# Attention's value products turned round, and the convolution's taps shared out anew, in a two-layer encoder kernel

## The chip, the cores and the metric

The kernel runs on one core of a Trainium2 chip. The metric is the device time of one execution in microseconds; the time before is the median of three runs. Engines go by their profile names: PE is TensorE (PEld its weight loads), DVE VectorE, ACT ScalarE, POOL GpSimd, SP SyncE, which here only issues transfers.

## What is computed

Two layers of a streaming encoder, on 512 tokens of 1024 features in float32. Each layer is a half-step feed-forward block, a mixing block, another half-step feed-forward block and a norm. The change lies in the mixing block:

```
h = rms_norm(x);  p = h @ w_in            # columns split among the two groups
group A: 8 heads of latent attention, q and k 96 wide, v 64 wide, block-causal mask
   probs = softmax(scores);  out = probs @ v
group B: u = a * sigmoid(g)               # 512 channels
   y = causal depthwise convolution of u, 31 taps, + bias
   conv = silu(layer_norm(y))
x = x + concat(attn, conv) @ w_out
```

So an output of the convolution at token t is the sum over s = 0..30 of tap s times u at token t - s, channel by channel.

## The kernel before

Features lie on the 128 partitions and the 512 tokens along the free axis, so x is eight tiles of 128 x 512. Large products are made in three passes over a high and a low part of both operands (`mm3`, L153 to L157). The order on each engine is set by a planner, which lists the instructions by simulated readiness and by their order in the program; `issue_after` adds constraints. Each engine then works through its list strictly in order.

The mixing block is `mix_body` (L617). It goes through these stages, all tiles of the step in one pass:
- The gated input u of the four convolution groups of 128 channels (`conv_in`, `glu`), the latent projections, queries and keys. `SEQ` (L44) gives their order; groups 2 and 3 come last. Weights come by SP's queue into three `raw` buffers, and ACT and DVE (or POOL) cut them into parts (`load_w`, L134).
- Attention (L808 to L908), a software pipeline over eight heads (`ORDER`, L59): `turn` transposes q and k; `scores` makes scores, maxima and exponentials for four blocks of 128 queries; `turn_p` transposes the probabilities, so that keys lie on the partitions; `values` (L861) takes each transposed 128 x 128 block of probabilities as the stationary operand and streams 64 value columns past it, ten products a head. An odd head then scales its pair by the reciprocal sums (L875), and `turn_out` (L879) transposes the pair's result back to features and splits it (L161, L162).
- The convolution (L913 to L933). `CONV = "DAAD"`: groups 0 and 3 lie on DVE, each tap one fused multiply-add in a PSUM tile `cv` (L922), copied back by ACT (L932). In groups 1 and 2 ACT makes the product of each tap (L926) and POOL adds it (L930). Only taps below `PAUSE` of group 1 may be added before the keys are done. These taps are spread by the planner among the attention's instructions.
- The layer norm over the 512 channels (L943 to L967): POOL sums the four groups (L944 to L946), a product with a constant matrix gives the mean of each token (L948), the groups are centred and squared, `token` and `spread` give the reciprocal deviation on all partitions (L198, L217), and the swish and the split give the four convolution operands.
- The output projection (L969 to L980). Its attention half can start without the convolution: `early_groups` (L936) fills PE during the layer norm. `E1 = 0`, `E2 = 2`, `E3 = 3` say how many of the early output columns come before the mean, before the norm's token sums and before the spread; `WOG = 3` is the number of output tiles worked on together. `WOP = 4` output weights are loaded during the attention.

SBUF tiles come from pools with a fixed number of buffers: `ring` (35 tiles of 128 x 512), `tmps` (5), the block's own `m` (12) and `y` (2), and seven PSUM banks beside `cv`.

Of the kernel before, what the change touches and what calls it, by code (L numbers as in the profile page):

```python
# [7 lines left out]
FP = mybir.dt.float32  # L8
# [17 lines left out]
DV = 64  # L26
# [3 lines left out]
CK = 31  # L30
# [29 lines left out]
JOINED = ("b21", "t3", "t4")  # L60

VECS = [("g1", 8), ("gm", 8), ("g2", 8), ("gp", 8), ("gql", 3), ("gkl", 2),
        ("cw", 4 * CK), ("cb", 4), ("lg", 4), ("lb", 4), ("gq", 1), ("gk", 1)]
VOFF = {}
_o = 0
for _n, _w in VECS:
# [1 line left out]
    _o += _w  # L68
VN = _o
CCOS, CSIN, CID = 0, 64, 128  # L70
CN = 256


@with_exitstack
def encoder_kernel(ctx: ExitStack, tc: tile.TileContext, xT, consts, vecs, rgain, wgu1, wd1, wdq1,
                   wcv, wql, wkl, wuq, wkv, wout, wgu2, wd2, wdq2, out):
    nc = tc.nc
# [18 lines left out]

    def bank():
        return psum.tile([P, S], FP, tag="ps", name=nm("ps"))
# [13 lines left out]
    ident = cst[:, CID:CID + P]  # L112
# [17 lines left out]
    def vv(l, name):  # L130
        o, w = VOFF[name]
        return vec[:, l, o:o + w]
# [18 lines left out]
    order = {}  # L151
# [7 lines left out]
    def split(src, made=slot):  # L159
        hi, lo = made(FR), made(FR)  # L160
        order["high"] = A.copy(hi, src).ins  # L161
        order["evicted"] = V.tensor_tensor(lo, src, hi.bitcast(FP), ALU.subtract).ins  # L162
        return hi, lo
# [452 lines left out]

    def mix_body(kpool, l, gx, norm, done):  # L617
        u, order = [], {}

        def kept(dt=FP):  # L620
            return kpool.tile([P, S], dt, tag="m", name=nm("m"), bufs=2 * WIDE)
        ys = [None if kind == "D" else kpool.tile([P, S], FP, tag="y", name=nm("y"), bufs=2) for kind in CONV]

        def glu(pa, pg):
            tg = tmp()
            V.tensor_tensor(tg, pg, R, ALU.mult)
            sg = tmp()
            order["gate"] = A.activation(sg, tg, AF.Sigmoid).ins
            ta = tmp()
            V.tensor_tensor(ta, pa, R, ALU.mult)  # L630
            uc = kept()
            (G if GLUP else V).tensor_tensor(uc, ta, sg, ALU.mult)
# [12 lines left out]
        stq = Stats()  # L645
        cqT, ckT, pq, scqs, vs = [], [], [], [], []
# [214 lines left out]
        def values(h):  # L861

            if h % 2 == 0:
                heads[h]["po"] = bank()
            po = heads[h - h % 2]["po"].rearrange("p (t h d) -> p t h d", t=NT, h=2)
            for t in range(NT):
                for j in range(t + 1):
                    T.matmul(po[:, t, h % 2], heads[h]["pt"][j][:, (t - j) * P:(t - j + 1) * P],  # L868
                             vs[j][:, h * DV:(h + 1) * DV], start=j == 0, stop=j == t)
# [5 lines left out]
            V.tensor_tensor(o.rearrange("p (t h d) -> p t h d", t=NT, h=2), po,  # L875
                            rs[:, :, :, None].to_broadcast([P, NT, 2, DV]), ALU.mult)
            heads[h]["o"] = o

        def turn_out(h):  # L879

            if h % 2 == 0:
                return
            o = heads[h]["o"]
            ps = bank()
            for t in range(NT):
                T.transpose(ps[:, t * P:(t + 1) * P], o[:, t * P:(t + 1) * P], ident)
# [9 lines left out]
        with tc.issue_after(order["turned"]):  # L896
            for t in range(NT):
                ps = up_kv(wv, t)
                v = kept()
                V.tensor_scalar(v, ps, sk[:, t:t + 1], None, ALU.mult)  # L900
                vs.append(v)
        with tc.issue_after(order["gate"]):
            scores(0)
        for step in range(H + 6):
            for stage, lag in STAGES:
                h = step - lag
                if 0 <= h < H and not (stage is turn and h < AHEAD or stage is scores and h == 0):
                    stage(h)  # L908
# [5 lines left out]
        for c in range(4):  # L914
            kind = CONV[c]
            acc = psum.tile([P, S], FP, tag="cv", name=nm("cv"), bufs=1) if kind == "D" else ys[c]
            tap = lambda k: cw[:, c * CK + k:c * CK + k + 1]
            A.activation(acc, u[c], AF.Identity, scale=tap(CK - 1), bias=cb[:, c:c + 1])  # L918
            for k in range(CK - 2, -1, -1):
                s = CK - 1 - k  # L920
                if kind == "D":
                    V.scalar_tensor_tensor(acc[:, s:], u[c][:, :S - s], tap(k), acc[:, s:], ALU.mult, ALU.add)  # L922
                    continue
                pr = kpool.tile([P, S], FP, tag="pr", name=nm("pr"), bufs=3)
                if kind == "A":
                    A.activation(pr[:, s:], u[c][:, :S - s], AF.Copy, scale=tap(k))  # L926
                else:
                    G.tensor_scalar(pr[:, s:], u[c][:, :S - s], tap(k), None, ALU.mult)
                with tc.issue_after(order["keys"]) if s >= PAUSE or c > 1 else nullcontext():
                    order["conv"] = G.tensor_tensor(acc[:, s:], acc[:, s:], pr[:, s:], ALU.add).ins  # L930
            if kind == "D":
                A.copy(u[c], acc)  # L932
                ys[c] = u[c]  # L933
        early = []

        def early_groups(ms):  # L936
# [9 lines left out]
        (G if YP else V).tensor_tensor(ysum, ysum, ys[3], ALU.add)  # L946
        pm = bank()
        T.matmul(pm, onesm, ysum, start=True, stop=True)  # L948
        if PRELOAD:
# [6 lines left out]
        r = st.token(CW)  # L956
        early_groups(range(E2, E3))
        pr = spread(r)
        early_groups(range(E3, WOG))
        lg, lb = vv(l, "lg"), vv(l, "lb")  # L960
        cv = []
        for c in range(4):
            z = tmp()
            V.tensor_tensor(z, ys[c], pr, ALU.mult)
            s = tmp()
# [275 lines left out]
```

## Time and profile before

| | |
|---|---|
| median of three runs | 1798.41 us (1798.37 to 1800.6) |
| profiled execution | 1798.87 us |
| its span on the core | 1797.1 us |
| granted TensorE clock | 1.0 |
| first mixing block, attention to convolution operands | about 450 to 521.5 us from the span's start |
| second mixing block, the same | about 1340 to 1411.5 us |

The profiled execution is one run with the hardware profiler on. A group row reads: line, engine, operation, output<-inputs, shape and count, then the busy time in us, the mean duration of one in ns, and the engine's idle time in us just before these instructions with what ended it. For PE the shape begins with rows*columns of the weight tile. Durations on PE run from entering the array to leaving it, so they overlap. A row of the chain in order of time reads: start, length, engine, tile and line, count.

### The profile page before, as it was taken

How to read it: one execution, taken by the hardware profiler on the slowest of the kernel's cores; microseconds unless marked ns; L12 is line 12 of the kernel's file. 1: busy time of each engine (PE TensorE's matmuls, PEld its weight loads, DVE VectorE, ACT ScalarE, POOL GpSimd, SP SyncE). 2: the span in 40 equal slices, each digit the busy share in tenths (PEclk: the TensorE clock that was granted, in tenths of full speed). 3: DMA queues.
4: the chain of work that ended last, by engine and by line, in shares of the span. 5: the costliest groups of instructions: out<-in, count | busy, mean ns of one | idle time of the engine just before them, and what ended most of it. 6: DMA issues, size and time to landing. Idle time of an engine off the chain costs nothing.

```text
span 1797.1 us, 29235 instructions
## 1 busy us (share of the span) xinstructions
PE 1781.8 (99%) x11334; PEld 1602.4 (89%) x11334; DVE 1494.5 (83%) x2299; ACT 1107.5 (62%) x1721; POOL 421.5 (23%) x343
## 2 busy tenths in 40 slices
PE   9999999999999999999999999999999999999998
PEld 7899999888788899999888999998978788999997
DVE  7898988589956989898779989876998668989883
ACT  5575756457953575756645757554779435756564
POOL 1000000258943000000310000002689410000002
PEclk9999999999999999999999999999999999999999
DMA  5657575325103466665426575743250125575742
GB/s 168 171 131 182 135 177 123 109 88 134 33 22 102 123 164 161 155 160 132 123 65 170 122 194 122 193 112 111 81 147 7 46 82 160 140 183 134 182 117 74
DMA packets 70413, 226.16 MB, mean 126 GB/s; under 512 B 7937, under 2 KB 8321, under 8 KB 70273
## 3 DMA queue, kind: packets, MB, share of 16 engines
q1 hardware_dynamic: 54000, 169.74, 30.3%
q0 software_dynamic: 16128, 54.53, 18.0%
q8 instruction: 89, 1.46, 0.3%
q14 instruction: 52, 0.42, 0.1%
q10 hardware_dynamic: 144, 0.00, 0.0%
HBM read 222.15 MB, written 2.10 MB: 125 GB/s over the span
## 4 chain that ended last, share of the span: by engine, by line
PE 91%; ACT 3%; DVE 2%; POOL 2%; issue 1%; DMA 0%; SPq 0%; ACTq 0%; POOLq 0%; DVEq 0%
PE ps L154 24%; PE ps L156 23%; PE ps L155 23%; PE ps L373 11%; PE ps L374 6%; PE ps L868 1%; PE ps L834 1%; POOL y L930 1%; ACT pr L926 1%; ACT r L840 1%; PE ps L855 1%; PE ps L198 0%; POOL sck L173 0%; PE ps L217 0%; DVE wl L246 0%
## 5 line engine op out<-in xcount | busy, mean ns | idle before, releaser
L155 PE MATMUL ps<-r,wh 128*128 128x256 f32 (+1 forms) x2540 | 806.8, 318 | 0.0
L154 PE MATMUL ps<-r,wh 128*128 128x256 f32 (+1 forms) x2540 | 803.6, 320 | 2.2 <-ACT wh L138 0.7
L156 PE MATMUL ps<-r,wl 128*128 128x256 f32 (+1 forms) x2348 | 749.2, 321 | 0.0
L154 PEld LDWEIGHTS ps<-r,wh 128*128 128x128 f32 x2540 | 480.5, 189 | 47.0 <-ACT wh L138 3.6
L155 PEld LDWEIGHTS ps<-r,wh 128*128 128x128 f32 x2540 | 481.6, 190 | 35.8 <-DVE r L162 1.5
L156 PEld LDWEIGHTS ps<-r,wl 128*128 128x128 f32 x2348 | 445.1, 190 | 33.5 <-DVE wl L144 0.4
L373 PE MATMUL ps<-xj,wh 128*128 128x512 f32 x864 | 303.9, 392 | 0.0
L138 ACT CAST wh<-raw 128x1024 fp32r<-128x1024 f32 (+3 forms) x148 | 131.9, 899 | 208.1 <-PE ps L155 125.8
L390 POOL DMA_DIRECT2D ls<-in_wgu x72 | 62.7, 871 | 734.7 <-ACT ls L389 595.3
L244 ACT CAST wh<-fr 128x1024 fp32r<-128x1024 f32 (+1 forms) x160 | 157.6, 985 | 104.4 <-DVE fr L410 53.2
L144 DVE TENSOR_TENSOR wl<-raw,wh 128x1024 fp32r<-128x1024 f32 (+3 forms) x132 | 145.3, 1108 | 91.3 <-ACT wh L138 90.9
L246 DVE TENSOR_TENSOR wl<-fr,wh 128x1024 fp32r<-128x1024 f32 (+1 forms) x160 | 182.3, 1139 | 20.3 <-ACT wh L244 20.3
L373 PEld LDWEIGHTS ps<-xj,wh 128*128 128x128 f32 x864 | 161.4, 188 | 30.1
L930 POOL TENSOR_TENSOR y<-y,pr 128x511 f32<-128x511 f32 (+14 forms) x120 | 158.6, 1322 | 54.5 <-ACT pr L926 47.1
L374 PE MATMUL ps<-xj,ls 128*128 128x256 f32 x576 | 161.3, 280 | 0.0
L244 ACT CAST wh<-raw 128x1024 fp32r<-128x1024 f32 (+1 forms) x100 | 98.2, 982 | 45.1 <-PE ps L155 24.2
L246 DVE TENSOR_TENSOR wl<-raw,wh 128x1024 fp32r<-128x1024 f32 (+1 forms) x100 | 113.5, 1135 | 14.2 <-ACT wh L244 13.7
L191 POOL TENSOR_TENSOR r<-r,t 128x512 f32<-128x512 f32 x45 | 75.0, 1676 | 175.6 <-ACT t L187 174.8
L374 PEld LDWEIGHTS ps<-xj,ls 128*128 128x128 f32 x576 | 108.3, 188 | 0.0
L389 ACT ACTIVATE ls<-fr 128x1024 fp32r<-128x1024 f32 (+1 forms) x56 | 56.1, 1002 | 74.5 <-PE ps L374 42.8
L926 ACT ACTIVATE pr<-m,vec 128x511 f32<-128x511 f32 (+14 forms) x120 | 85.7, 736 | 13.2 <-POOL y L930 13.2
L922 DVE SCALAR_TENSOR_TENSOR cv<-m,vec,cv 128x511 f32<-128x511 f32 (+14 forms) x120 | 87.8, 732 | 3.6 <-ACT cv L918 2.2
(241 smaller groups left out, 2944.9 us busy)
## 6 DMA issues: line engine op xcount, KB each, us to landing
fr<-in_wgu SPq DMA_DIRECT2D x112, 512.0 KB, 4.2
ls<-in_wgu POOLq DMA_DIRECT2D x72, 512.0 KB, 6.2
raw<-in_wgu SPq DMA_DIRECT2D x62, 512.0 KB, 4.5
fr<-in_wdq SPq DMA_DIRECT2D x48, 384.0 KB, 4.6
ls<-in_wdq POOLq DMA_DIRECT2D x32, 384.0 KB, 4.8
raw<-in_wd SPq DMA_DIRECT2D x32, 384.0 KB, 3.2
raw<-in_wd SPq DMA_DIRECT2D x32, 256.0 KB, 2.8
raw<-in_wcv SPq DMA_DIRECT2D x16, 512.0 KB, 3.6
```

Of the source, the lines that this page charges most:

```text
L138: order["cast"] = A.copy(hi[:, :w], raw[:, :w]).ins
L144: (G if kind in POOLW.split() else V).tensor_tensor(lo[:, :w], raw[:, :w], hi[:, :w].bitcast(FP), ALU.subtract)
L154: T.matmul(o, lh, rh, start=first, stop=False, skip_group_check=free)
L155: T.matmul(o, lh, rl, start=False, stop=False, skip_group_check=free)
L156: order["mm"] = T.matmul(o, ll, rh, start=False, stop=last, skip_group_check=free).ins
L244: A.copy(hi[:, :w], src[:, :w])
L246: order["lo"] = V.tensor_tensor(lo[:, :w], src[:, :w], hi[:, :w].bitcast(FP), ALU.subtract).ins
L373: T.matmul(o, w[0][:, c], both, start=start and k == 0, stop=False, skip_group_check=True)
L374: last = T.matmul(o[:, 0:HS], w[1][:, c], both[:, 0:HS], start=False, stop=k == 3, skip_group_check=True).ins
L922: V.scalar_tensor_tensor(acc[:, s:], u[c][:, :S - s], tap(k), acc[:, s:], ALU.mult, ALU.add)
L926: A.activation(pr[:, s:], u[c][:, :S - s], AF.Copy, scale=tap(k))
L930: order["conv"] = G.tensor_tensor(acc[:, s:], acc[:, s:], pr[:, s:], ALU.add).ins
```

## The change

- **Values.** `values` now handles a pair of heads at its odd head. The value tile of a head (64 columns) is the stationary operand and the transposed probabilities stream past it: 4 products a head of 512, 384, 256 and 128 columns. The two heads write partitions 0 to 63 and 64 to 127 of one bank, in alternation. The result has features on the partitions at once, so the four transposes in `turn_out` go. The reciprocal sums are needed along the free axis then: 8 products of a broadcast column with the identity spread them, ACT copies them to SBUF, and DVE multiplies.
- **Taps.** `TAPS = (0, 31, 31, 9)` gives for each group the number of taps that are not on DVE. Group 0 is on DVE as before, group 1 on ACT and POOL. Of group 2 (`PC`) the first 16 taps (`PT`) go to PE and 15 stay on ACT and POOL. Of group 3 the first 9 taps go to ACT and POOL and 22 stay on DVE in `cv`, begun by an ACT copy and added to the group by DVE at the end.
- **Taps on PE.** For 32 channels at a time, four copies of u shifted by 0 to 3 tokens are brought by 4 transfers on SP's queue into one 128-row tile (16 transfers a layer). `diag` holds the taps as 32-column diagonal blocks, made by POOL. `conv_pe` makes 16 products of 500 to 512 columns, in four 32-row parts of one bank, in alternation, and ACT adds the bias. It stands ahead of pipeline step 3 (`PSTEP`).
- **Smaller edits.** The last add of the layer norm's sum goes from POOL to DVE. `E1` is 1 and `WOG` 4: one early column before the mean, two before the token sums, three before the spread and a fourth after it, and the output tiles go four and four. Pool `m` has 11 buffers, `y` 3; three of the four pairs' results take ring tiles, before it was two.

```diff
-CONV = "DAAD"
+TAPS = (0, 31, 31, 9)
+Q = 32
+PT = 16
+PC = 2
+PSTEP = 3
...
-E1 = 0
-YP = 1
+E1 = 1
 E2 = 2
 E3 = 3
-WOG = 3
+WOG = 4
...
+        diag = kpool.tile([P, PT, Q], FP, tag="m", name=nm("m"), bufs=11)
+        G.tensor_tensor(diag, cst[:, None, CI32:CI32 + Q].to_broadcast([P, PT, Q]),
+                        vv(l, "cp")[:, :, None].to_broadcast([P, PT, Q]), ALU.mult)
+        shifted = []
...
             glu(*pp)
+            if c != PC:
+                return
+            for i in range(4):
+                v = slot()
+                V.memset(v[:, 0:4], 0.0)
+                for r in range(4):
+                    nc.sync.dma_start(out=v[r * Q:(r + 1) * Q, r:], in_=u[c][i * Q:(i + 1) * Q, 0:S - r])
+                shifted.append(v)
+
+        def conv_pe():
+
+            ps = bank()
+            for a in range(PT // 4):
+                for i in range(4):
+                    T.matmul(ps[i * Q:(i + 1) * Q, 4 * a:], diag[:, 4 * a + i], shifted[i][:, 0:S - 4 * a],
+                             start=a == 0, stop=a == PT // 4 - 1)
+            A.activation(ys[PC], ps, AF.Identity, bias=vv(l, "cb")[:, PC:PC + 1])
...
             if h % 2 == 0:
-                heads[h]["po"] = bank()
-            po = heads[h - h % 2]["po"].rearrange("p (t h d) -> p t h d", t=NT, h=2)
-            for t in range(NT):
-                for j in range(t + 1):
-                    T.matmul(po[:, t, h % 2], heads[h]["pt"][j][:, (t - j) * P:(t - j + 1) * P],
-                             vs[j][:, h * DV:(h + 1) * DV], start=j == 0, stop=j == t)
-            if h % 2 == 0:
                 return
             rs = small.tile([P, NT, 2], FP, tag="rs", name=nm("rs"))
             V.reciprocal(rs, heads[h - 1]["sums"])
+            pr = bank()
+            for t in range(NT):
+                for i in range(2):
+                    T.matmul(pr[i * DV:(i + 1) * DV, t * P:(t + 1) * P], rs[:, t, i:i + 1].to_broadcast([P, DV]),
+                             ident, start=True, stop=True)
+            r = tmp()
+            A.copy(r, pr)
+            po = bank()
+            for j in range(NT):
+                for i in range(2):
+                    T.matmul(po[i * DV:(i + 1) * DV, j * P:], vs[j][:, (h - 1 + i) * DV:(h + i) * DV],
+                             heads[h - 1 + i]["pt"][j], start=j == 0, stop=j == NT - 1)
             o = tmp()
-            V.tensor_tensor(o.rearrange("p (t h d) -> p t h d", t=NT, h=2), po,
-                            rs[:, :, :, None].to_broadcast([P, NT, 2, DV]), ALU.mult)
+            V.tensor_tensor(o, po, r, ALU.mult)
...
-            ps = bank()
-            for t in range(NT):
-                T.transpose(ps[:, t * P:(t + 1) * P], o[:, t * P:(t + 1) * P], ident)
-            at.append(split(ps, kept if len(at) < 2 else slot))
+            at.append(split(heads[h]["o"], kept if len(at) < 1 else slot))
...
+            if step == PSTEP:
+                conv_pe()
...
+            acc = psum.tile([P, S], FP, tag="cv", name=nm("cv"), bufs=1) if n < CK else None
+            if n and c != PC:
+                A.activation(ys[c], u[c], AF.Identity, scale=tap(CK - 1), bias=cb[:, c:c + 1])
+            for s in range(n, CK):
+                k = CK - 1 - s
+                if s == 0:
+                    A.activation(acc, u[c], AF.Identity, scale=tap(k), bias=cb[:, c:c + 1])
+                elif s == n:
+                    A.activation(acc[:, s:], u[c][:, :S - s], AF.Copy, scale=tap(k))
+                else:
                     V.scalar_tensor_tensor(acc[:, s:], u[c][:, :S - s], tap(k), acc[:, s:], ALU.mult, ALU.add)
+            for s in range(PT if c == PC else 1, n):
...
+                A.activation(pr[:, s:], u[c][:, :S - s], AF.Copy, scale=tap(k))
                 with tc.issue_after(order["keys"]) if s >= PAUSE or c > 1 else nullcontext():
-                    order["conv"] = G.tensor_tensor(acc[:, s:], acc[:, s:], pr[:, s:], ALU.add).ins
-            if kind == "D":
+                    order["conv"] = G.tensor_tensor(ys[c][:, s:], ys[c][:, s:], pr[:, s:], ALU.add).ins
+            if not n:
                 A.copy(u[c], acc)
                 ys[c] = u[c]
+            elif n < CK:
+                V.tensor_tensor(ys[c][:, n:], ys[c][:, n:], acc[:, n:], ALU.add)
...
-        (G if YP else V).tensor_tensor(ysum, ysum, ys[3], ALU.add)
+        V.tensor_tensor(ysum, ysum, ys[3], ALU.add)
```

More of the change, by code (lines that the diff above doesn't have):

```diff
@@ L70 @@
 CCOS, CSIN, CID = 0, 64, 128
-CN = 256
+CI32 = 256
+CN = 288
 @with_exitstack
@@ L618, in mix_body @@
         u, order = [], {}
+        diag = kpool.tile([P, PT, Q], FP, tag="m", name=nm("m"), bufs=11)
+        G.tensor_tensor(diag, cst[:, None, CI32:CI32 + Q].to_broadcast([P, PT, Q]),
+                        vv(l, "cp")[:, :, None].to_broadcast([P, PT, Q]), ALU.mult)
+        shifted = []
         def kept(dt=FP):
-            return kpool.tile([P, S], dt, tag="m", name=nm("m"), bufs=2 * WIDE)
-        ys = [None if kind == "D" else kpool.tile([P, S], FP, tag="y", name=nm("y"), bufs=2) for kind in CONV]
+            return kpool.tile([P, S], dt, tag="m", name=nm("m"), bufs=11)
+        ys = [kpool.tile([P, S], FP, tag="y", name=nm("y"), bufs=3) if n else None for n in TAPS]
         def glu(pa, pg):
@@ L913, in mix_body @@
         cw, cb = vv(l, "cw"), vv(l, "cb")
[L914 to L916 removed]
+        for c, n in enumerate(TAPS):
             tap = lambda k: cw[:, c * CK + k:c * CK + k + 1]
[L918 to L921 removed]
+            acc = psum.tile([P, S], FP, tag="cv", name=nm("cv"), bufs=1) if n < CK else None
[8 more added lines that the diff above has]
+                else:
                     V.scalar_tensor_tensor(acc[:, s:], u[c][:, :S - s], tap(k), acc[:, s:], ALU.mult, ALU.add)
[L923 removed]
+            for s in range(PT if c == PC else 1, n):
+                k = CK - 1 - s
                 pr = kpool.tile([P, S], FP, tag="pr", name=nm("pr"), bufs=3)
[L925 to L928, printed above, removed]
+                A.activation(pr[:, s:], u[c][:, :S - s], AF.Copy, scale=tap(k))
                 with tc.issue_after(order["keys"]) if s >= PAUSE or c > 1 else nullcontext():
[L930 to L931 removed]
+                    order["conv"] = G.tensor_tensor(ys[c][:, s:], ys[c][:, s:], pr[:, s:], ALU.add).ins
+            if not n:
                 A.copy(u[c], acc)
                 ys[c] = u[c]
+            elif n < CK:
+                V.tensor_tensor(ys[c][:, n:], ys[c][:, n:], acc[:, n:], ALU.add)
         early = []
@@ L1205 @@
     put("cw", a["conv_w"].reshape(L, CK, 4, P).transpose(3, 0, 2, 1).reshape(P, L, 4 * CK))
+    cp = a["conv_w"][:, ::-1][:, :PT, PC * P:(PC + 1) * P].reshape(L, PT // 4, 4, 4, Q)
+    put("cp", cp.transpose(2, 4, 0, 1, 3).reshape(P, L, PT))
     for name, key in (("gq", "q_norm"), ("gk", "k_norm")):
@@ L1219 @@
     consts[:, CID:CID + P] = np.eye(P, dtype=f32)
+    consts[:, CI32:CI32 + Q] = np.tile(np.eye(Q, dtype=f32), (4, 1))
     arrays = {
```

3 lines of the change are left out of this document (1 added, 2 removed).

## The prediction

> **What bounds the kernel now.** I read the page first, for the share of each engine and the chain that ended last.
>
> ```profile
> span 1797.1 us, 29235 instructions
> PE 1781.8 (99%) x11334; PEld 1602.4 (89%) x11334; DVE 1494.5 (83%) x2299; ACT 1107.5 (62%) x1721; POOL 421.5 (23%) x343
> ...
> PE 91%; ACT 3%; DVE 2%; POOL 2%; issue 1%; DMA 0%; SPq 0%; ACTq 0%; POOLq 0%; DVEq 0%
> ```
>
> PE is busy for 99% of the span and carries 91% of the chain: the time is TensorE's work plus about 15 us in which it stands idle. Every edit lies in the mixing stage, which comes twice. So next I took a table by stage: attention from its first exponentials to its last products (450 to 505, and 1340 to 1395), and the stretch behind it, up to the first output products of the convolution half.
>
> ```profile
> core 0: us, PE busy (x) PEld busy (x) DVE busy (x) ACT busy (x) POOL busy (x), PEclk, DMA share, GB/s
> ...
> 450.00:505.00 55.00, 53.09 (x387) 43.12 (x385) 49.27 (x97) 50.48 (x122) 50.62 (x42) 1.00 0.11 24
> 505.00:521.50 16.50, 15.59 (x76) 12.03 (x74) 9.37 (x16) 6.47 (x11) 2.51 (x3) 1.00 0.00 0
> ...
> 1340.00:1395.00 55.00, 53.55 (x392) 43.77 (x391) 48.75 (x95) 50.50 (x122) 50.55 (x42) 1.00 0.11 22
> 1395.00:1411.50 16.50, 15.23 (x70) 11.43 (x69) 9.15 (x15) 6.62 (x11) 3.23 (x3) 1.00 0.00 0
> ```
>
> In the attention stretch all four engines are busy for 49 to 54 of 55 us. PE leads by 3 us; the others are full because the convolution's taps lie there. A cut on PE alone would soon meet ACT and POOL, and a cut on those alone would meet PE. The clock is granted in full (1.00), so no work runs slowly.
>
> **What the touched PE work costs.** From the groups by line and, for the pace, the chain in order of time around the end of the first attention (start, length, what):
>
> ```profile
> L834 PE MATMUL ps<-r,r 96*128 96x384 f32 (+3 forms) x128 | 45.3, 464 | 2.9 <-ACT r L840 2.7
> ...
> L868 PE MATMUL ps<-m,r 128*128 128x64 f32 x320 | 39.6, 273 | 0.0
> L217 PE MATMUL ps<-t,ones 128*128 128x512 f32 x18 | 9.0, 591 | 0.0
> L886 PE MATMUL ps<-cst,t 128*128 128x128 f32 x32 | 5.0, 279 | 1.6 <-DVE t L875 1.6
> L948 PE MATMUL ps<-t,onesm 128*128 128x512 f32 x4 | 2.1, 619 | 0.4 <-POOL t L946 0.4
> ...
> L811 PEld LDWEIGHTS ps<-cst,q 128*96 128x96 f32 x64 | 6.7, 127 | 3.2 <-ACT r L840 1.8 <-DVE cv L922 0.3 <-issue 0.3
> ```
>
> ```profile
> 500.23 1.10 PE ps L855 x10
> ...
> 503.95 2.19 PE ps L868 x20
> 506.17 0.70 DVE t L875
> 506.91 0.66 PE ps L886 x4
> 507.57 0.86 PE ps L948 x2
> 508.43 0.23 PE ps L154
> ...
> 518.58 0.70 DVE t L964
> ...
> 520.79 0.61 ACT r L161
> 521.45 1.20 PE ps L154 x4
> ```
>
> The duration 273 ns is a single record's way through the array; the pace is what counts. Twenty value records take 2.19 us, 0.11 us each, although each streams only 64 columns. Two 512-column records take 0.86 us, 0.43 each, or 0.84 ns a column, so a 128-column record also takes 0.11. A float32 product is two records (L217: nine calls, 18 records; L868: 160 products, 320 records); a transpose is one, also at 0.11 (1.10 us for ten).
>
> Removed, over both layers: 320 value records at 0.11 = 35.0, and 32 transposes of the output at 0.11 = 3.5. Together 38.5 us.
>
> Added, if every record ran alone:
> - Reciprocal sums spread over 64 rows: 8 products for each of 8 pairs of heads, 128 records of 128 columns at 0.11 = 14.1.
> - Values with the roles exchanged: for each head, products of 512, 384, 256 and 128 columns, 1280 columns at 0.84 ns = 1.08 us per pass; 16 heads, two records each, 32 passes = 34.4.
> - Convolution: 16 products a layer of 500 to 512 columns, 64 records at 0.43 = 27.5.
>
> That is 76.0, a loss of 37.5 us. But neighbouring products of the new code fill different columns of the array: two halves in the values, four quarters in the convolution, with the tile index innermost. If they run side by side in full, the cost is 14.1/2 + 34.4/2 + 27.5/4 = 31.1, a gain of 7.4; if at most two records run at a time, 38.0, a gain of 0.5. No weight tile of this profile is narrower than the 96 columns of L811, which tell nothing of two tiles at once, so both ends stay open. I take full overlap, since such neighbours write different rows of PSUM and load different columns.
>
> [...]
>
> [...]
>
> Waits that go: the transposes' 1.6 for L875 and the mean's 0.4 for POOL, 2.0. What is late next is the last pair's split, 0.70 + 0.61 + 0.7 us behind its last value product; the first early output group, now ahead of the mean, has nine products that do not need it (2.1 us), and hides it.
>
> **The other engines, per layer.**
>
> ```profile
> L930 POOL TENSOR_TENSOR y<-y,pr 128x511 f32<-128x511 f32 (+14 forms) x120 | 158.6, 1322 | 54.5 <-ACT pr L926 47.1
> ...
> L926 ACT ACTIVATE pr<-m,vec 128x511 f32<-128x511 f32 (+14 forms) x120 | 85.7, 736 | 13.2 <-POOL y L930 13.2
> L922 DVE SCALAR_TENSOR_TENSOR cv<-m,vec,cv 128x511 f32<-128x511 f32 (+14 forms) x120 | 87.8, 732 | 3.6 <-ACT cv L918 2.2
> ```
>
> ```profile
> L223 ACT COPY r<-ps 128x512 f32<-128x512 f32 x7 | 4.1, 589 | 1.5 <-PE ps L217 1.4
> ...
> L918 ACT ACTIVATE cv<-m,vec 128x512 f32<-128x512 f32 x4 | 3.1, 773 | 0.6 <-DVE m L632 0.6
> L932 ACT COPY m<-cv 128x512 f32<-128x512 f32 x4 | 2.6, 656 | 0.0
> ```
>
> ```profile
> L954 DVE TENSOR_TENSOR y<-y,ps 128x512 f32<-128x512 f32 x4 | 2.6, 680 | 0.0
> ...
> L122 DVE MEMSET onesm<- 128x128 f32 x1 | 0.2, 165 | 0.0
> ```
>
> ```profile
> L191 POOL TENSOR_TENSOR r<-r,t 128x512 f32<-128x512 f32 x45 | 75.0, 1676 | 175.6 <-ACT t L187 174.8
> ...
> L946 POOL TENSOR_TENSOR t<-t,m 128x512 f32<-128x512 f32 x2 | 2.5, 1267 | 0.2
> ```
>
> Taps on ACT and POOL go from 60 to 53: 30 of the second group, 15 of the third, 8 of the last.
> - POOL: 7 adds at 1.32 less, and the last add of the sum moves away: 10.5 us less; a product for the diagonals (between L946's 1.27 and L191's 1.68 us) comes at the start of the stage, hidden in POOL's long waits for ACT (L191).
> - DVE: 30 taps of the last group become 21, and two adds come (0.68 each): 5.2 less. Four memsets, at most L122's 165 ns each, take it back to 4.5.
> - ACT: 7 products at 0.74 less, one copy (0.66) less, four copies of the spread reciprocals (0.59) and one scaled copy (0.77) more: 2.7 less.
>
> So ACT is relieved least, and the convolution's sum is ready about 2.7 us earlier. PE gains (7.4 - 3.3 + 2.0)/2 = 3.0 per layer. The two keep pace, and I let neither cut the other.
>
> **Transfers.** The shifted copies are 16 transfers a layer on SP's queue, waiting for the third group's gate.
>
> ```profile
> 386.25 0.33 SPq L136 DMA_DIRECT2D raw<-in_wuq  x1
> ...
> 424.07 20.99 SPq L136 DMA_DIRECT2D raw<-in_wout  x6
> ```
>
> ```profile
> ls<-in_wgu POOLq DMA_DIRECT2D x72, 512.0 KB, 6.2
> ...
> raw<-in_wd SPq DMA_DIRECT2D x32, 256.0 KB, 2.8
> ```
>
> ```profile
> 437.38 0.69 DVE L632 TENSOR_TENSOR m<-t,t 128x512 f32<-128x512 f32 x1
> ```
>
> An issue takes 0.33 us, 5.3 for sixteen. The gate is done at 438.1, and the loads that could stand behind them are the output weights, not needed before the early groups at 508.43. Even behind all of those (445) they are issued by 450.4. The page's loads land in 2.8 to 6.2 us; with that as the bound the copies are there by 457. The convolution products stand behind two steps of heads that only begin about 450, and at 55/8 = 6.9 us a head reach PE some 10 us later at the least. I cost them at nothing; if they came late, the whole attention would wait behind them on PE, microsecond for microsecond. The regrouping into 4 + 4 output columns costs nothing either: the chain shows four products side by side (x4 at 521.45) already.
>
> **Sum.** 1798.87 us (the profiled execution; its span is 1797.1, 1.8 lies around it) - 7.4 + 3.3 - 2.0 = 1792.8. The median of the runs is 0.5 below the profiled execution, so the prediction is 1792.3.
>
> **Rivals.**
> - *Two at a time.* The two records of one float32 product need the same columns. If PE starts records strictly in order, the second record of a tile holds up the next tile, and four quarters run no better than two halves. For it: the records of L868 and L217 come in pairs. Against it: nothing here shows that order binds across tiles. Time: 1798.87 - 0.5 + 3.3 - 2.0 - 0.5 = 1799.2. [...]
> - *No overlap (slower).* Narrow float32 tiles take turns, and the change then doesn't do what its order is laid out for. PE pays 37.5 + 3.3 - 2.0 over the run: 1837.2. It decides as soon as the added 76.0 is cut by less than about half, since 38.5 was removed.
> - *The norm's chain rules.* From the mean's product (507.57) to the first products of the convolution half (521.45) 13.9 us pass. PE covered that with four early groups of 12 records at 0.23 (the pace at 508.43); one of them now goes ahead of the mean, so 2.8 per layer lie open unless the mean's product comes that much earlier. For it: the stretch 505 to 521.5 is already short of 0.9 us of PE. Against it: the sum should be ready 2.7 earlier. If the mean's product stays where it is, PE's saving is lost there: 1798.4; if it also stands behind the first group's wait for the last split, up to 1 us a layer more.
>
> **How the numbers follow.** Forecast 0.55, two at a time 0.22, no overlap 0.12, norm's chain 0.11. The forecast's own range is 1786 to 1796: passages free (-3.3) and ACT's early waits in the attention (L834's 2.7) gone too, against passages at double price (+3.3). With two at a time and the norm's chain, passages again at both ends, 1784 to 1803 holds 0.85 or so; only no overlap lies outside. A measurement of this kernel tells about 0.2%, 3.6 us, from no change. Faster by more: most of the forecast (0.48) and a little of the two middle rivals, 0.53. Within: 0.06 of the forecast, two thirds of the middle rivals, 0.26. Slower: no overlap and the upper ends of the others, 0.21.
>
> **What would show it.** Starts of the two half-tile value products within one another's duration, and convolution records closer than 0.43 us: at 0.11 full overlap, at 0.21 two at a time, at 0.43 none. The transposes of the output and their wait are gone. The gap from the mean's product to the first convolution half stays near 14 us; if PE stands idle in it, the norm's chain rules. POOL's last add should end some 10 us ahead of PE's last value product, or ACT is the bound. The prediction is wrong if PE waits on the copies, or if narrow tiles do not overlap.

## The result and the profile after

The changed kernel took 1858.07 us (median of four runs, 1857.51 to 1859.27) against 1799.05 (1798.37 to 1800.6) before: a ratio of 1.0328, 95% interval 1.031 to 1.0346. It is slower by 59 us, and the time lies far above the range. One execution of all those reported below, of the kernel with `E1 = 0` alone, took 3550.61 us and is left out of its ratio.

The head of the page of the kernel after:

```profile
span 1857.5 us, 29229 instructions
...
PE 1785.9 (96%) x11302; PEld 1583.9 (85%) x11302; DVE 1473.3 (79%) x2293; ACT 1108.7 (60%) x1715; POOL 389.4 (21%) x329
...
PEclk9999999999969999999999999999999799999999
```

Two of the forty slices of the granted clock, one in each mixing block, are no longer 9. A slice is 46 us, so a 6 or 7 means that the clock was at half for most of one. The next view, what PE waited for (total us, times, longest), shows the place:

```profile
PE ps L979 <- DVE t L977: 54.9, 2, 27.5
```

L979 is the mean's product. Before, it waited 0.4 us in all; now it waits 27.5 us in each layer. The place in time, from the unfiltered timeline of after:

```profile
533.61 1.24 POOL L959 TENSOR_TENSOR y<-y,pr 128x504 f32<-128x504 f32 x1
534.88 0.68 DVE L964 TENSOR_TENSOR y<-y,cv 128x503 f32<-128x503 f32 x1 [26.71 <-POOL y L959]
535.60 0.69 DVE L977 TENSOR_TENSOR t<-t,y 128x512 f32<-128x512 f32 x1
...
536.43 2.04 PE L979 MATMUL ps<-t,onesm 128*128 128x512 f32 x2 [27.47 <-DVE t L977]
```

Read from the bottom up: PE waits for the convolution's sum, DVE for POOL's last tap. POOL's last tap ends at 534.85; the last value product had left PE at 505.6, 29 us before. The stretches around it (us, then busy time and count of PE, PEld, DVE, ACT, POOL, the granted clock, DMA share, GB/s):

```profile
500.00:509.00 9.00, 7.73 (x44) 4.23 (x40) 3.39 (x5) 5.82 (x10) 8.92 (x7) 1.00 0.00 0
509.00:536.00 27.00, 0.00 (x0) 0.00 (x0) 1.08 (x2) 13.32 (x18) 24.67 (x21) 0.51 0.00 0
536.00:540.00 4.00, 3.56 (x7) 2.18 (x8) 1.77 (x4) 0.96 (x3) 0.00 (x0) 0.50 0.00 0
```

For 27 us PE does nothing and POOL is busy almost without a pause, and 4 us more pass at half clock once PE may go on. The mean's product is the milestone by which the kernels can be compared. Its rows before and after (durations min/median/max in ns, then the first and the last start, the weight loads first):

```profile
L948 PEld LDWEIGHTS ps<-t,onesm x4: 186/190/192, 507.3 to 1397.4; 128*128 128x128 f32 x4
L948 PE MATMUL ps<-t,onesm x4: 592/594/697, 507.4 to 1397.9; 128*128 128x512 f32 x4
...
L979 PEld LDWEIGHTS ps<-t,onesm x4: 285/310/333, 536.4 to 1457.3; 128*128 128x128 f32 x4
L979 PE MATMUL ps<-t,onesm x4: 1061/1126/1191, 536.4 to 1458.1; 128*128 128x512 f32 x4
```

It starts at 507.4 us before and at 536.4 after, 29 later; in the second layer its last weight load starts at 1397.4 and 1457.3, 60 later; the spans differ by 60.4. So nearly the whole loss is there when the second mean starts, about half of it from each layer. Not all of it is waiting: the two waits are 54.9 us, and the half clock lasts 4 to 5 us beyond each of them, some 4 us lost in the two layers.

Had POOL too much work? Its group row of after stands in the page as

```profile
L959 POOL TENSOR_TENSOR y<-y,pr 128x511 f32<-128x511 f32 (+29 forms) x106 | 134.1, 1270 | 28.0 <-ACT y L945 20.1
```

There are 53 adds a layer, as counted, and they are shorter than before (1270 ns against 1322). The new thing is the last field: 20.1 us idle for L945, the scaled first tap of a group, which all its adds wait for. Tile `y`, before and then after (durations min/median/max in ns, then the first and the last start):

```profile
L930 POOL TENSOR_TENSOR y<-y,pr x120: 1206/1255/2092, 382.9 to 1392.1; 128x511 f32<-128x511 f32 x4, 128x510 f32<-128x510 f32 x4, 128x509 f32<-128x509 f32 x4, 128x508 f32<-128x508 f32 x4
L918 ACT ACTIVATE y<-m,vec x4: 800/810/817, 381.4 to 1328.5; 128x512 f32<-128x512 f32 x4
```

```profile
L959 POOL TENSOR_TENSOR y<-y,pr x106: 1203/1242/1776, 461.5 to 1454.3; 128x511 f32<-128x511 f32 x4, 128x510 f32<-128x510 f32 x4, 128x509 f32<-128x509 f32 x4, 128x508 f32<-128x508 f32 x4
...
L945 ACT ACTIVATE y<-m,vec x4: 801/802/802, 460.6 to 1382.1; 128x512 f32<-128x512 f32 x4
L666 ACT ACTIVATE y<-ps,vec x2: 687/687/687, 460.0 to 1380.8; 128x512 f32<-128x512 f32 x2
```

Before, group 1 begins at 381.4 and its adds at 382.9. After, they begin at 460.6 and 461.5, 79 us later, directly behind L666, the result of the products on PE. POOL has to put 53 adds of 1.27 us, 67 us, one after another behind that point, and 461.5 + 67, two adds of the sum (2.5) and 3.5 of pauses and other work give the 535 seen. What was counted was the work that leaves POOL; what was not looked at is when the work that stays may begin.

### The profile page after: what moved, and what is told of

Its sections match the earlier page's. It is cut to its first block, busy times and chain, and to the rows that moved or that the text cites. A ratio compares the mean times of both kernels' runs of the same rounds, so it can differ in the third digit from the quotient of the medians.

```text
span 1857.5 us, 29229 instructions
## 1 busy us (share of the span) xinstructions
PE 1785.9 (96%) x11302; PEld 1583.9 (85%) x11302; DVE 1473.3 (79%) x2293; ACT 1108.7 (60%) x1715; POOL 389.4 (21%) x329
## 4 chain that ended last, share of the span: by engine, by line
PE 55%; POOL 2%; ACT 2%; DVE 2%; issue 0%; ACTq 0%; POOLq 0%; DVEq 0%
PE ps L158 14%; PE ps L160 14%; PE ps L159 14%; PE ps L377 7%; PE ps L378 4%; POOL y L959 2%; ACT pr L957 1%; ACT r L865 1%; PE ps L859 0%; DVE wl L250 0%; PE ps L202 0%; PE ps L664 0%; PE ps L221 0%; DVE x L484 0%; PE ps L1063 0%
## 5 line engine op out<-in xcount | busy, mean ns | idle before, releaser
L148 DVE TENSOR_TENSOR wl<-raw,wh 128x1024 fp32r<-128x1024 f32 (+3 forms) x132 | 139.5, 1066 | 88.6 <-ACT wh L142 88.1
L959 POOL TENSOR_TENSOR y<-y,pr 128x511 f32<-128x511 f32 (+29 forms) x106 | 134.1, 1270 | 28.0 <-ACT y L945 20.1
L250 DVE TENSOR_TENSOR wl<-raw,wh 128x1024 fp32r<-128x1024 f32 (+1 forms) x100 | 113.5, 1135 | 14.2 <-ACT wh L248 13.8
L957 ACT ACTIVATE pr<-m,vec 128x511 f32<-128x511 f32 (+29 forms) x106 | 75.8, 739 | 32.3 <-POOL y L959 26.6
L394 POOL DMA_DIRECT2D ls<-in_wdq x32 | 27.6, 863 | 262.9 <-ACT ls L393 262.9
```

The source lines that it names most:

```text
L148: (G if kind in POOLW.split() else V).tensor_tensor(lo[:, :w], raw[:, :w], hi[:, :w].bitcast(FP), ALU.subtract)
L250: order["lo"] = V.tensor_tensor(lo[:, :w], src[:, :w], hi[:, :w].bitcast(FP), ALU.subtract).ins
L394: G.dma_start(out=lo[:, :n], in_=w, accum_op=ALU.add)
L959: order["conv"] = G.tensor_tensor(ys[c][:, s:], ys[c][:, s:], pr[:, s:], ALU.add).ins
```

## The experiments

**The theory.** The three groups' sums share the tag `y`. The planner seems to hand out the buffers of one tag in the program's order of first writes. In the program, `conv_pe` writes group 2's sum at pipeline step 3, and group 1's first tap stands behind the whole pipeline, so that ACT's list puts it behind L666, 79 us late. The planner's inside was not looked at; the experiments test what follows from this. **Rivals:** the narrow tiles do not overlap and PE pays; ACT or POOL is simply too busy; the end of the stage (E1, the add on DVE) makes the loss. Ratios are to the kernel before, with their 95% intervals.

### A buffer of its own for the result of PE

```diff
-ys = [kpool.tile([P, S], FP, tag="y", name=nm("y"), bufs=3) if n else None for n in TAPS]
+ys = [kpool.tile([P, S], FP, tag="yp" if c == PC else "y", name=nm("y"), bufs=1 if c == PC else 2) if n else None
+      for c, n in enumerate(TAPS)]
```

> The changed kernel with one edit: the result of the convolution products on TensorE gets a buffer of its own in place of one of the three shared with the bases of groups 1 and 3. Theory (the order in which shared buffers are handed out): group 1's base is then written near 375 us again and its first 15 adds on GpSimd lie ahead of the keys, as before; the 27 us in which TensorE waits for the mean in each layer go, and the time is 1785 to 1797. Rival (the taps are simply too much work for ScalarE and GpSimd in the attention): the base's place does not matter, and the time stays above 1840.

Measured: 1806.68 us, ratio 1.0041 (1.0029 to 1.0054). Tile `y` of this kernel:

```profile
L960 POOL TENSOR_TENSOR y<-y,pr x106: 1206/1256/2091, 382.6 to 1389.0; 128x511 f32<-128x511 f32 x4, 128x510 f32<-128x510 f32 x4, 128x509 f32<-128x509 f32 x4, 128x508 f32<-128x508 f32 x4
...
L946 ACT ACTIVATE y<-m,vec x4: 804/811/817, 381.1 to 1344.8; 128x512 f32<-128x512 f32 x4
L667 ACT ACTIVATE y<-ps,vec x2: 687/689/691, 463.6 to 1356.9; 128x512 f32<-128x512 f32 x2
```

The number of buffers is the same, the adds start at 382.6 again, and 51 of the 59 us are gone. But the kernel is still 7 us above before, not below it, where the theory expected it. A second cause is left. The timeline of this kernel around the mean:

```profile
509.34 0.69 DVE L906 TENSOR_TENSOR t<-ps,t 128x512 f32<-128x512 f32 x1 [4.21 <-PE ps L903]
...
510.72 0.69 DVE L166 TENSOR_TENSOR r<-t,r 128x512 fp32r<-128x512 f32 x1 [0.68 <-ACT r L165]
510.74 0.49 PE L158 MATMUL ps<-r,wh 128*128 128x512 f32 x1 [0.61 <-ACT r L165]
511.33 0.69 DVE L978 TENSOR_TENSOR t<-t,y 128x512 f32<-128x512 f32 x1
511.46 0.50 PE L159 MATMUL ps<-r,wh 128*128 128x512 f32 x1 [0.23 <-DVE r L166]
```

The last add of the sum (L978), moved to DVE, stands on DVE's list behind the last pair's scaling and split, and begins at 511.33. The sum of the first three groups was done on POOL at 502.3 (its last add starts at 501.04 and takes 1.28), nine microseconds earlier. And PE's early output group, moved ahead of the mean, waits for the same split (0.61 and 0.23). The mean starts at 512.2, 5 later than before; then PE runs dry behind it, as the list of its waits shows:

```profile
PE ps L202 <- DVE r L195: 4.2, 2, 2.1
```

L202 is the norm's token sums. That is the rival "the norm's chain" in the prediction. Besides, 10.2 us of its mixing blocks pass at half clock (5.1 lost), 6.8 of them at the convolution block (last section) and 3.4 behind the wait for L202 in the first layer.

### Late first tap in the kernel before

```diff
+        with tc.issue_after(heads[3]["q"]) if c == 1 else nullcontext():
             A.activation(acc, u[c], AF.Identity, scale=tap(CK - 1), bias=cb[:, c:c + 1])
```

Nothing else of the change is in this kernel.

> The kernel before with one constraint more: group 1's base on ScalarE may be listed only behind the copy of head 3's transposed queries. Nothing else is changed. Theory (the late base alone makes the loss): TensorE waits 25 to 35 us for the mean in each layer, and the time is 1845 to 1870. Rival (the planner finds other work, and the loss needs the new taps too): below 1815.

Measured: 1871.35 us, ratio 1.04 (1.0381 to 1.0419), a little above what was expected. From the row of tile `y` (group 1's first tap at 457.7) and the waits of PE:

```profile
L919 ACT ACTIVATE y<-m,vec x4: 806/806/807, 457.7 to 1384.7; 128x512 f32<-128x512 f32 x4
...
PE ps L949 <- POOL t L947: 71.8, 2, 35.9
```

Starting group 1 as late as in after is enough to make the loss, without narrow tiles and without products on PE. It is larger here (72 us), in keeping with 60 adds a layer behind the late point in place of 53: 7 adds of 1.24 us are 8.7, and each wait is 8.4 longer.

### Same tag, first tap written earlier in the program

This kernel has the later version of the stage's end (see "Both moved back"), three buffers of one tag as in after, and group 1's first tap written right after its gate.

```diff
+            if c == 1:
+                A.activation(ys[1], u[1], AF.Identity, scale=vv(l, "cw")[:, 2 * CK - 1:2 * CK], bias=vv(l, "cb")[:, 1:2])
...
-            if n and c != PC:
+            if n and c not in (1, PC):
```

> As e7_both, but the three results share their buffers again as in the changed kernel, and group 1's base is written, in the program, right behind group 1's gate, ahead of the convolution products on TensorE. Theory (shared buffers are handed out in the program's order of first writes): the base is early again and the time is that of e7, 1791 to 1797. Rival (sharing the buffers is itself what delays the base): above 1840.

Measured: 1792.41 us, ratio 0.996 (0.9946 to 0.9974). From tile `y`:

```profile
L651 ACT ACTIVATE y<-m,vec x2: 815/816/817, 380.8 to 1267.6; 128x512 f32<-128x512 f32 x2
```

The first tap runs at 380.8. The time is that of the same version with a buffer of its own ("Both moved back", 1793.78). Sharing the tag is not the harm; the order of the first writes is. With the first experiment this fixes the cause: own tag or earlier write, either one suffices.

### Narrow products listed tile by tile

On top of the buffer of its own, the loops are exchanged so that all products of one tile of the array follow one another (three places):

```diff
-            for a in range(PT // 4):
-                for i in range(4):
+            for i in range(4):
+                for a in range(PT // 4):
```

> As e1_own_slot, but the narrow products are listed tile by tile (all of one half or quarter, then the next) in place of in turn; same products, same results. Theory (the overlap needs neighbours on different columns): the values' records run at 0.11 to 0.43 us each and the convolution's at 0.43, 20 to 40 us more than e1. Rival (the overlap does not hang on the order): within 3 us of e1.

Measured: 1829.56 us, ratio 1.0166 (1.0152 to 1.018), 23 us above the same kernel with tiles in alternation. PE's timeline with tiles in alternation (the kernel "both moved back"), one convolution block and one pair of heads:

```profile
456.07 3.60 PE L665 MATMUL ps<-r,m 128*32 128x512 f32 x32
459.61 0.70 PE L860 MATMUL ps<-r,r 96*128 96x256 f32 x2
...
500.51 1.09 PE L896 MATMUL ps<-cst,rs 128*64 128x128 f32 x16
501.43 2.32 PE L903 MATMUL ps<-r,m 128*64 128x512 f32 x16
503.69 0.70 PE L980 MATMUL ps<-t,onesm 128*128 128x512 f32 x1
```

and tile by tile:

```profile
457.13 10.47 PE L665 MATMUL ps<-r,m 128*32 128x512 f32 x32
467.53 0.70 PE L860 MATMUL ps<-r,r 96*128 96x256 f32 x2
...
496.93 1.25 PE L896 MATMUL ps<-cst,rs 128*64 128x128 f32 x13
497.91 0.64 PE L903 MATMUL ps<-r,m 128*64 128x512 f32 x1
498.02 0.49 PE L896 MATMUL ps<-cst,rs 128*64 128x128 f32 x3
498.39 3.45 PE L903 MATMUL ps<-r,m 128*64 128x512 f32 x15
501.77 0.70 PE L860 MATMUL ps<-r,r 96*128 96x256 f32 x2
```

Count from one block's first record to the next block's: in alternation 32 convolution records of 500 to 512 columns take 459.61 - 456.07 = 3.54 us, 0.111 each, where one alone costs 0.43. The pair of heads takes 503.69 - 500.51 = 3.18. Tile by tile they take 10.40 (3.4 us of it at half clock, so 8.7 at full) and 4.84. Over two convolution blocks and eight pairs that is 2 x 5.2 + 8 x 1.66 = 23.7 us, the 23 measured. In these float32 products the overlap is full where neighbours lie in different columns: 0.111 us a record, where a quarter of 0.43 is 0.108.

The expectation had the convolution's records at 0.43 us tile by tile; 8.7 us are 0.27 each. The second layer, all at full clock, shows why (1362.06 to 1370.79, 8.73 us). Each tile has eight records. The next tile's first record (512 columns) starts at 1363.80, together with the fifth record of the tile before (504 columns) and ahead of its last three, which start at 1364.22, 1364.64 and 1365.06. So the last records of a tile run beside the first ones of the next, though the program lists them one behind the other.

### The values alone

The change's `values` and `turn_out` in the kernel before; taps and the end of the stage stay as they were.

> The kernel before with the turned value products alone; taps, buffers and early groups as before. Theory (narrow tiles overlap): TensorE loses 35.0 + 3.5 us of records and gains about 25, so 6 to 13 us less, if the convolution's sum does not become the later one; 1786 to 1793. Rival (the convolution's sum already ends with the attention, and nothing relieves ScalarE here, which has four more copies a layer): within 3 us of before.

Measured: 1806.54 us, ratio 1.0038 (1.0024 to 1.0052): slower, where the theory expected a gain and the rival no change. Of its waits and stretches:

```profile
PE ps L948 <- POOL t L946: 11.0, 2, 6.1
```

```profile
505.00:508.00 3.00, 0.00 (x0) 0.00 (x0) 0.83 (x1) 1.88 (x2) 2.84 (x3) 1.00 0.00 0
508.00:515.00 7.00, 6.02 (x12) 4.11 (x13) 3.78 (x6) 2.66 (x5) 0.92 (x1) 0.52 0.00 0
515.00:520.00 5.00, 5.00 (x27) 4.16 (x27) 0.85 (x2) 0.00 (x0) 0.41 (x1) 0.99 0.01 3
```

PE is done with the values earlier, but POOL is not done with the sum. What PE saved it now waits (4.8 us up to 508.98, 6.1 in the second layer), and with that wait the granted clock falls to half (508.3 to 515.1) and stays there into the early groups behind the mean. The mean itself starts 1.6 us later than before in the first layer. A saving that runs into a wait for another engine is worth nothing by itself, and the half clock and the later sum turn it into a loss; how the 7 us divide between these two was not tried.

### The end of the stage: three kernels

All three have the buffer of its own. First, the last add back on POOL, with the early group still ahead of the mean:

```diff
-        V.tensor_tensor(ysum, ysum, ys[3], ALU.add)
+        G.tensor_tensor(ysum, ysum, ys[3], ALU.add)
```

> e1_own_slot with the last add of the norm's sum back on GpSimd; the first early output group stays ahead of the mean. In e1 TensorE starts the mean at 512.2 us in the first layer, though the sum's first two adds end at 502.3: the third stands on VectorE behind the last pair's scaling and split. Theory (both edits hold the mean, each alone suffices): the mean still stands on TensorE behind the first early group, whose last third needs that split; 1 to 3 us less than e1, 1803 to 1806. Rival (the add on VectorE alone holds it): 10 us or more less than e1, below 1797.

Measured: 1806.46 us, ratio 1.0035 (1.0021 to 1.0049). No gain, and just above the range expected: the early group ahead of the mean still waits for the split (0.61 us), 2.1 us for L202 remain in each layer, and in the first layer 6.8 us at half clock begin at the end of that wait.

Second, no early group ahead of the mean (`E1 = 0`), the add still on DVE:

> e1_own_slot with no early output group ahead of the mean (E1 = 0); the last add of the sum stays on VectorE. Theory (each alone suffices): the mean waits for the add behind the last pair's split, about 2 us earlier than in e1, but the first early group now fills the norm; 1800 to 1806. Rival (the early group ahead of the mean alone holds it): below 1797.

Measured: 1801.93 us, ratio 1.0015 (1.0006 to 1.0025), 4.8 us less than with the early group. Now the mean's product itself waits for DVE's add:

```profile
PE ps L980 <- DVE t L978: 5.9, 2, 2.9
```

Third, both moved back:

```diff
-E1 = 1
+E1 = 0
-WOG = 4
+WOG = 3
-        V.tensor_tensor(ysum, ysum, ys[3], ALU.add)
+        G.tensor_tensor(ysum, ysum, ys[3], ALU.add)
```

> e1_own_slot with the smaller edits undone: last add of the sum on GpSimd, no early group ahead of the mean, output tiles three and three. Theory: the mean starts right behind the last value product, near 506 us in the first layer, four groups fill the norm, and the time is 1786 to 1796, faster than before by 3 to 12 us. Rival (the taps and values themselves cost the 7 us): within 3 us of e1.

Measured: 1793.78 us, ratio 0.9972 (0.9961 to 0.9983). The mean starts at 503.7, 3.7 earlier than before, and nothing waits for it. From the timeline of POOL, the last add of the sum before, and the last two of this kernel:

```profile
505.29 1.27 POOL L946 TENSOR_TENSOR t<-t,m 128x512 f32<-128x512 f32 x1
...
498.14 1.28 POOL L977 TENSOR_TENSOR t<-t,y 128x512 f32<-128x512 f32 x1
499.49 1.27 POOL L978 TENSOR_TENSOR t<-t,y 128x512 f32<-128x512 f32 x1
```

The sum is ready at 500.8, where it was ready at 506.6 before, and PE gets to it at 503.7. Alone, the add moved back gave 0.2 us and the early group taken away 4.8; both together, with `WOG`, give 12.9. So the add on DVE and the early group hide the harm of each other. Of the 12.9, 5.1 are the half clock of the kernel with the buffer of its own, 3.4 of it at the convolution block, 50 us ahead of the stage's end; here the clock stays full through both mixing blocks. Why the wait there became shorter was not traced. `WOG` was not changed alone. The step from the second of these kernels is 8.2 us by the medians and 7.1 between the profiled executions; its wait of 5.9 and a half-clock stretch of 3.4 us (1.7 lost) make 7.6, so little is left for it.

### The taps alone, and the values without the taps

Both start from "both moved back". Taps alone: `values` and `turn_out` as before the change.

> As e7_both, but with the value products and output transposes of the kernel before: the new sharing of the taps alone. Theory (TensorE bounds the attention): it pays the convolution's products, some 4.4 us a layer where they overlap four at a time, and gains nothing from the other engines being done earlier: 1803 to 1810. Rival (the other engines bound it): at or below 1796.

Measured: 1803.88 us, ratio 1.0025 (1.0015 to 1.0035).

The other: `conv_pe` out, its 16 taps back on ACT and POOL, the nine taps and the values as in the change.

> As e7_both, with the 16 taps of group 2 on ScalarE and GpSimd as before and no convolution product on TensorE: 30 adds and products more. Theory (GpSimd's list sets the mean): 15 adds at 1.3 us make the sum some 19 us later in each layer, of which the slack of the last pairs hides little: 1815 to 1835. Rival (TensorE bounds the attention): TensorE saves its 4 us a layer, 1785 to 1790.

Measured: 1830.23 us, ratio 1.0171 (1.0157 to 1.0185). Of PE's waits:

```profile
PE ps L979 <- POOL t L977: 35.6, 2, 18.2
```

With the end of the stage as before the four corners are now: neither part 1799, values alone 1806.5, taps alone 1803.9, both 1793.8. Each alone loses and the two together gain: the taps free POOL at PE's cost (7 us of products), and the values then give PE the time that POOL no longer needs.

### What sets the end now: two more

The sum and the mean written ahead of the last pair's values, so that PE could do the mean earlier (the block of taps, sum and mean moved to pipeline step 11, unchanged in itself):

> As e7_both, with the taps, the norm's sum and the mean written ahead of the last pair's value products in the program, so that the mean may go to TensorE before them. Same work. Theory (the norm's chain of about 14 us behind the mean still sets the end of the stage): the last value products go beside that chain, 1 to 3 us less a layer than e7: 1787 to 1792. Rival (TensorE's own work sets the end by now): within 1.5 us of e7.

Measured: 1793.29 us, ratio 0.9966 (0.9953 to 0.9978). The mean runs at 500.5 instead of 503.7 and the end stays within 0.5 us: the gain of 1 to 3 us a layer did not come, and the rival holds. It is PE's own work that counts there.

The nine taps of the last group back on DVE:

```diff
-TAPS = (0, 31, 31, 9)
+TAPS = (0, 31, 31, 0)
```

> As e7_both, with all taps of the last group on VectorE again (TAPS 0, 31, 31, 0): 16 adds and 16 products fewer on GpSimd and ScalarE, 16 fused taps more on VectorE. Theory (GpSimd's list ends last, VectorE is done 20 us before the mean): within 2 us of e7. Rival (VectorE would be late without the nine taps): 4 us or more above e7.

Measured: 1793.9 us, ratio 0.997 (0.9958 to 0.9982). No difference: once POOL is done 3 us before PE asks, whether DVE has 21 or 30 taps there does not show.

## Why the prediction was wrong, point by point

- **The step that failed** is "the convolution's sum is ready about 2.7 us earlier", and with it "the two keep pace". It was worked out from instructions taken off ACT, POOL and DVE; the sum was ready 27 us after PE asked for it because the first add of group 1 moved from 382.9 to 461.5. The counts and durations were right (53 adds, 1.27 us). With the start mended and the end of the stage as before, the sum is indeed ready earlier, by 5.8 us (500.8 against 506.6). The step treated relief as if it moved the end of a chain, and took for granted that the chain starts when it did. Shown by three kernels: own tag (51 us back), earlier first write (as good as an own tag), late first tap in the old kernel (+72).
- **What could have been seen.** The row of tile `y` before: adds of 1.25 us from 382.9 on, 84 us ahead of the first value product (467.2). That early start was a part of the schedule, and the change puts another first write of the same tag ahead of it in the program. Both facts of the change, `y` with three buffers and `conv_pe` ahead of step 3, stand in its description.
- **The rival "the norm's chain rules"** was real, with both its causes, and too small: priced at 6 to 8 us over the run against 13 measured between the first and the last version of the stage's end, of which 3.4 are half clock that arose ahead of it. Its cost was taken from PE's cover and up to 1 us a layer for the first group's wait; the add that had been moved to DVE, behind the last pair's scaling and split, was counted at 0.68 us and not by its place in DVE's list. The statement that nine products which do not need the last split hide it was nearly right: of some 2 us PE still waited 0.6 and 0.2.
- **A cost not in the sum**: around PE's waits the granted clock was at half for 3.4 to 37.5 us at a time, in after for 30.7 us at each wait of 27.5; shorter waits differ (last section). No run shows this term alone.
- **PE's terms were right.** Full overlap, not two at a time and not none: 0.111 us per quarter-tile record against the 0.11 predicted. Strict order, on which the rival "two at a time" rested, did not bind: in after, from 454.76, four records start 7 ns apart, read as the first ones of the four tiles, and only then the second ones, 0.45 us later. Tile by tile, the next tile's first record (1363.80) even starts between the two records of one product of the tile before (504 columns, 1363.80 and 1364.22). Added up in the kernel "both moved back" from each such record's start to the next record's, at most 0.6 us each, sums (7.7), values (18.2) and convolution (7.1) make 32.9 us with their passages, against 31.1 + 3.3 = 34.4 predicted. The 3.3 are the author's price for those passages, into and out of the blocks of narrow tiles: 20 times 273 - 110 = 163 ns, a record's duration less its pace in before. No run shows this term alone; the blocks as a whole came to 1.8 us above the 31.1.
- **The copies came in time.** SP's own timeline in after has

```profile
435.49 13.84 SPq L656 DMA_DIRECT2D r<-m  x16
```

so the sixteen took 13.8 us to issue, not 5.3, and were out by 449.3; PE never waited for them. The waits that were to go (transposes, POOL) are in no list of the kernel "both moved back".
- **The sum.** With the two causes undone the kernel takes 1793.8 us by the median, where the sum said 1792.3: a gain of 5.2 us in the profiled execution against 6.1 forecast. What makes the difference between these two, and the 1.5 us by which the blocks were cheaper than priced, was not traced. In the chances, two thirds of the two middle rivals' 0.33 are 0.22, so "within" comes to 0.28, not 0.26; nothing here hangs on it.
- **The list of what would show it** held the sign that failed: POOL's last add 10 us ahead of PE's last value product. It ended 29 us behind (with the start mended and the end as before, 10.6 ahead: 493.1 and 503.7). But the list blamed ACT's load for such a case, and of its two conditions of failure neither came true. That an engine relieved of work might start later was not on it.

## What to carry to other kernels

For each chain that a change relieves, ask first when its first instruction may run and what the new code puts ahead of it: a shared buffer tag, a list in program order, a queue. Count work only after that. And test the parts of a change in pairs as well as alone: here each half lost 5 to 7 us by itself and both together, with the start mended, gained 5 to 7.

The lowest median is that of the change with group 1's first tap written right after its gate, the sum's last add on POOL, no early group ahead of the mean and output tiles in threes: 1792.41 us, 0.996 (0.9946 to 0.9974) of before. Three other versions with that end of the stage lie at 1793.29 to 1793.9, and their intervals overlap with it.

## What the runs showed of the chip

**The clock was at half around some short waits.** In the kernel with the buffer of its own, PE waits 1.39 us for ACT just before 454.73. The stretches around it:

```profile
450.00:455.00 5.00, 3.61 (x21) 2.26 (x20) 4.77 (x10) 5.00 (x10) 4.49 (x5) 1.00 0.72 177
455.00:462.00 7.00, 6.86 (x30) 1.89 (x33) 6.10 (x10) 6.46 (x18) 6.28 (x6) 0.54 0.90 259
```

The clock is half from 455.5 to 462.3, 6.8 us, while PE is busy throughout, and the convolution block takes 5.82 us instead of 3.54. In the kernel "both moved back" the longest wait at that place is 1.1 us and no drop follows (1.00 from 455 to 462). The length of a wait alone did not decide here. In the kernel with the buffer of its own, the wait of 2.1 us for L202 was followed by 3.4 us of half clock in the first layer and by none in the second; tile by tile, by none in the first and 3.4 us in the second. With `E1 = 0` alone, a wait of 2.9 us went with none in the first layer and with 3.4 us, begun half a microsecond before its end, in the second. Within the mixing blocks the lengths of half clock seen (3.4, 6.8, 17.1, 20.5, 30.7 and 37.5 us) each lie within 0.1 us of a whole multiple of the shortest.

**The float32 products shared the array fully.** Four quarter tiles ran 3.9 times as fast as one after another (0.111 us a record against 0.43), and two halves took about the time of one (3.18 us for both heads' sums and values, where the values of a single head alone were priced at 2.15 and its sums at 0.88).
